# A hybrid decoder block on one core: the start re-staged with the first scale on TensorE, centring by rounded products, and another order

## The chip, the cores and the metric

The kernel runs on one core of a Trainium2 chip. The core has a matrix engine (PE, with its weight loads shown apart as PEld), a vector engine (DVE), an activation engine (ACT), a general engine (POOL) and a queue engine (SP), which here issues the loads and stores. The metric is the device time of one execution in microseconds (us); shorter is better. Three timed executions of the kernel before gave 963.92, 964.54 and 966.73 us, so its median is 964.54 us.

## The reference, cut to what matters

All arrays are fp32; there is one sequence of S = 1024 tokens and D = 1024 channels. The vector `c` conditions every stage by shifts, scales and gates.

```python
c_act = jax.nn.silu(c)
cond = c_act @ ada_w[i] + ada_b[i]
shift1, scale1, gate1, shift2, scale2, gate2 = jnp.split(cond, N_MOD, axis=-1)

h = modulate(rmsnorm(x, norm1_g[i]), shift1, scale1)      # h*(1+scale)+shift
z = h @ w_in[i] + b_in[i]                                 # 1024 -> 2048
u, v, val, gate = jnp.split(z, [D_A, 2 * D_A, 2 * D_A + D_B], axis=-1)
y_a = spatial_gating_mixer(gelu(u), gelu(v), ...)         # chunks of 128 tokens, 8 heads
y_b = conformer_conv_mixer(val, gate, ...)                # 31 taps, then a group norm, silu
y = jnp.concatenate([rmsnorm(y_a, ...), rmsnorm(y_b, ...)], axis=-1)
x = x + gate1[:, None, :] * (y @ w_out[i])

h2 = modulate(rmsnorm(x, norm2_g[i]), shift2, scale2)
g_ff, up_ff = jnp.split(h2 @ w_ffn_in[i], 2, axis=-1)     # 1024 -> 2 x 2816
x = x + gate2[:, None, :] * ((jax.nn.silu(g_ff) * up_ff) @ w_ffn_out[i])

shift_f, scale_f = jnp.split(c_act @ ada_f_w + ada_f_b, 2, axis=-1)
return modulate(rmsnorm(x, norm_f_g), shift_f, scale_f)
```

The group norm of the convolution branch subtracts, over 64 channels, the mean, and divides by the deviation. The matrix `gcen` (128x128) does the subtraction as a product: it is the identity less 1/64 within a group.

## The kernel before, in words

Channels lie on the partitions and tokens along the free axis, so `x` is eight tiles of 128 channels; the tokens are worked in two halves of 512. A product of two fp32 matrices is made of rounded parts: each operand is split into a value rounded to fp32r (`h`, `wh_...`, the "high" part) and the remainder (`wl_...`, and a second plane of `h`), and three fp32r products are added up in a bank (`mm3`, L748): high by high (L750), low weight by high (L751), high weight by low (L752). A true fp32 matrix product is used only for small things, such as sums of squares and the group norm's centring (L1090).

The stages, as the trace places them: the start (0 to 16 us: loads of `x`, the sums of squares, the first reciprocal root, the first scale and shift); phase 1 of half 0 (16 to 61 us: for k = 0 to 7 a scale, a shift, a weight tile and 24 products into eight banks `p`); the remaining input projections `u`, `vg`, `v` with the convolution of half 0, whose taps run on DVE as one multiply-add each (`cv`, L1070); the spatial gate, the branch norms and the output projection of half 0; then "ahead" products (`ah`, L1139), products of the FFN's first layer that need only half 0 and that are interleaved with the convolution and the group norms of half 1 (257 to 345 us); the output projection of half 1; a stretch in which the second half's FFN operand is prepared (385 to 446 us); the dense FFN (446 to 940 us); and the tail.

A shift or a scale column is a dot product of `c_act` with 128 rows of `ada_w`. Its usual form (`ada_cols`, L693) loads these rows as a 128x1024 tile and lets DVE multiply and sum up in one instruction (SCALAR_TENSOR_TENSOR at L703); some are done by POOL's multiply (L700) with ACT's sum (L701).

What sets the order of the work: the program is first written in plain order, and then a planner in the kernel (`fix_order`, L561) fixes the order of every engine's instructions. It holds a graph of the instructions with a duration for each, goes forward and backward through it by a list rule, and stretches every duration off PE by a margin (one factor for computing, one for DMAs). The kernel before makes twelve orders, four rounds for each of three margins, replays each four times with jittered durations, and keeps the one with the smallest sum of replayed times. Extra edges say what must come first: `in_turn` chains the first loads on SP's queue, and `issue_after` holds an instruction behind another.

The loads at the start are issued as `c_row`, four tiles of 512 KB of `x` (two channel blocks each), the first scale's rows, the first shift's rows, the first weight tile and `colt` (small columns: biases, norm gains, convolution taps). The squares of `x` are made by turns on ACT (even k) and DVE (odd k); PE sums them over the channels into `ssq_n1_0` (L890); ACT takes the root (L894), DVE the reciprocal (L895), PE spreads the row over the partitions (L897), DVE multiplies `x` by it (`t_h`, L926), and ACT applies scale and shift and rounds (`h`, L928). `keep_busy` (L873) puts idle bf16 products of 128x512 behind the sums so that PE doesn't stand still.

Around 119 us the first product of the `v` projection needs a bank that the spatial bias' sums (`rs`) still hold; the four DVE instructions at L860 read it into `bst`.

Of the kernel before, what the change touches and what calls it, by code (L numbers as in the profile page):

```python
# [13 lines left out]
P = 128  # L14
S = 1024
D = 1024
# [19 lines left out]
IDLE = (1, 1, 2, 3, 3)  # L36
# [9 lines left out]
    ("ada_b", 64), ("norm1_g", 8), ("norm2_g", 8), ("norm_f_g", 8), ("b_in", 16),  # L46
# [31 lines left out]
MARGINS = ((1.01, 1.05), (1.015, 1.075), (1.02, 1.1))  # L78
JITTER = (0.008, 0.08)
TRIALS = 4  # L80
# [421 lines left out]
def replay(g, order):  # L502

    place, done, at = dict.fromkeys(ENGINES, 0), {}, [0.0] * len(g.steps)
    need = [len(s.before) for s in g.steps]
    slots, clock, table = Slots(g), Clock(True), None
    for _ in range(len(g.steps)):
        best = None
        for e in ENGINES:
            if place[e] == len(order[e]) or need[order[e][place[e]].n]:  # L510
                continue
            s = order[e][place[e]]
            tag, t = slots.blocked_on(s)
            t = max(t, at[s.n], clock.free[e])
            if tag is None and (best is None or t < best[0]):
                best = t, s
        t, s = best
        slots.take(s)
        if s.table not in (None, table):
            table, t = s.table, t + TABLE_LOAD  # L520
        begin, end = clock.run(s, t)
        done[s.n] = end
        if slots.release(s, end + SIGNAL[s.engine]):
            slots.hand_over()
        for n in s.after:
            need[n] -= 1
            if (s.n, n) in g.turns:
                at[n] = max(at[n], t + DMA_ISSUE)
            elif g.steps[n].engine == s.engine and not s.dma:
                at[n] = max(at[n], clock.free["PE"] if s.engine == "PE" else end)  # L530
            else:
                at[n] = max(at[n], end + SIGNAL[s.engine])
        place[s.engine] += 1
    return max(done.values())


# [16 lines left out]
def jittered(g, order, seed):  # L553

    import random
    rng = random.Random(seed)
    with stretched(g, lambda s: 1 + abs(rng.gauss(0, JITTER[s.dma]))):
        return replay(g, order)


def fix_order(tc, edges, stacked, reusing, rounds=4):  # L561

    g = Graph(list(tc.nc.cur_bb.bb.instructions), edges, stacked, reusing)
    orders = []
    for margin in MARGINS:
        with stretched(g, lambda s: margin[s.dma]):
            order, done, follows = forward(g, list(range(len(g.steps))))
            for _ in range(rounds):
                tail = backward(g, [-t for t in done], follows)
                order, done, follows = forward(g, [-t for t in tail])  # L570
                orders.append(order)
    times = [sum(jittered(g, order, seed) for seed in range(TRIALS)) for order in orders]
    best = orders[times.index(min(times))]
    for steps in best.values():
# [7 lines left out]
def block_kernel(ctx: ExitStack, tc: tile.TileContext, xT, c, ada, cols, vbias, bs, wsp,  # L582
# [49 lines left out]
    c_load = nc.sync.dma_start(c_row[0:1, :], c).ins  # L632
# [19 lines left out]
    sel_tok = const.tile([P, 4], F32, name="sel_tok")  # L652
    V.memset(sel_tok, 0.0)
    for q in range(4):
        V.memset(sel_tok[32 * q:32 * q + 1, q:q + 1], 1.0)

    warm = const.tile([P, 1], F32, name="warm")
    A.activation(warm, epst, AF.Silu)
    cact = const.tile([P, D], F32, name="cact")
# [986 lines left out]
```

## Time and profile before

| what | value |
|---|---|
| timed executions | 963.92, 964.54, 966.73 us (median 964.54) |
| the profiled execution | 967.9 us, of it span 965.8 us |
| mean granted clock of PE in it | 0.995 |
| PE busy | 946.5 us, 98% of the span |
| DVE busy | 861.9 us, 89% |
| ACT busy | 482.1 us, 50% |
| POOL busy | 413.6 us, 43% |
| moved by DMA | 184.24 MB, mean 191 GB/s |

Every number of a stage comes from the profiled execution, which is 3.4 us longer than the median; the part of its time that lies outside the span is 2.1 us. A row of the timeline view gives start, duration, engine, line, operation, tiles, and in brackets how long the engine stood idle ahead of it and what released it; a row with "x3" holds three instructions one behind another. A row of the windows view gives the stretch and its length, then each engine's busy time with its instructions in it, then the clock granted to PE, the share of DMA engines busy and the GB/s. A row of the waits view gives what waited for what: total us, times, longest us.

### The profile page before, as it was taken

To read this page: it belongs to the slowest core of one execution; us is meant where nothing else is said; L and a number is where in the kernel's file an instruction comes from. 1 tells how busy PE (TensorE), PEld (TensorE's weight loads), DVE (VectorE), ACT (ScalarE), POOL (GpSimd) and SP (SyncE) were. 2 spreads that over 40 slices of the span, in tenths; PEclk is the share of its full clock that TensorE was granted. 3 is DMA by queue.
4 is the path that set the end of the run, shared out by engine and by line. 5 is a ranking of instruction groups with operands and counts; after the bars stand their busy time and mean duration, and the time that the engine had idled before them with its cause. 6 is when DMAs were issued, how large, how long until landed. Compare 5 with 4: busy or idle time off the path is not lost.

```text
span 965.8 us, 12863 instructions
## 1 busy us (share of the span) xinstructions
PE 946.5 (98%) x4461; PEld 767.1 (79%) x4461; DVE 861.9 (89%) x1226; ACT 482.1 (50%) x770; POOL 413.6 (43%) x253
## 2 busy tenths in 40 slices
PE   7999999999999999999999999999999999999996
PEld 4888777778777788887888888888888888888885
DVE  6989999999999763899999999999778989969966
ACT  6778468763474743554333333223337337227426
POOL 0069896776554403673545454554534200000132
PEclk9999999999999999999999999999999999999998
DMA  9873342443385443753677677767648848405104
GB/s 351 325 265 136 110 174 88 153 159 130 139 280 202 147 146 138 263 205 119 239 238 251 221 236 243 249 236 238 224 171 277 269 158 260 164 33 165 54 1 174
DMA packets 70498, 184.24 MB, mean 191 GB/s; under 512 B 7841, under 2 KB 8353, under 8 KB 70434
## 3 DMA queue, kind: packets, MB, share of 16 engines
q1 hardware_dynamic: 70434, 183.43, 55.0%
q8 instruction: 35, 0.57, 0.3%
q14 instruction: 29, 0.24, 0.1%
HBM read 142.24 MB, written 41.16 MB: 190 GB/s over the span
## 4 chain that ended last, share of the span: by engine, by line
PE 84%; DVE 9%; DMA 2%; ACT 2%; issue 2%; POOL 1%; SPq 0%; POOLq 0%; ACTq 0%; DVEq 0%
PE B L1139 31%; PE C L1139 18%; PE ah L1139 9%; PE A L1139 3%; PE po L752 3%; PE po L751 3%; PE po L750 3%; DVE cv L1070 2%; PE p L752 2%; PE p L750 2%; PE p L751 2%; PE v L750 2%; PE v L752 1%; DVE ada L703 1%; PE v L751 1%
## 5 line engine op out<-in xcount | busy, mean ns | idle before, releaser
L1139 PE MATMUL B<-h,w_f 128*128 128x512 f32 x816 | 189.9, 389 | 0.6 <-ACT w_f L1131 0.3
L1139 PEld LDWEIGHTS B<-h,w_f 128*128 128x128 f32 x816 | 153.1, 188 | 33.0 <-ACT w_f L1131 0.8
L1070 DVE SCALAR_TENSOR_TENSOR cv<-ypad,colt,cv 128x512 f32<-128x512 f32 x216 | 147.8, 745 | 0.3
L1139 PE MATMUL B<-fa,w_d 128*128 128x512 f32 x528 | 125.0, 389 | 0.0
L1139 PE MATMUL C<-h,w_f 128*128 128x512 f32 x528 | 123.7, 389 | 0.0
L1139 PEld LDWEIGHTS C<-h,w_f 128*128 128x128 f32 x528 | 99.1, 188 | 20.9 <-ACT w_f L1131 0.3
L1139 PEld LDWEIGHTS B<-fa,w_d 128*128 128x128 f32 x528 | 99.0, 188 | 20.9 <-DVE x L1500 0.3
L1139 PE MATMUL ah<-h,wh_a 128*128 128x512 f32 x320 | 101.3, 394 | 0.0
L1426 POOL TENSOR_TENSOR sq_nf<-sq_nf,sq_nf 128x512 f32<-128x512 f32 (+1 forms) x15 | 17.4, 1163 | 170.9 <-ACT sq_nf L1420 170.8
L1131 ACT ACTIVATE w_f<-raw_f 128x512 fp32r<-128x512 f32 x68 | 42.4, 630 | 87.8 <-PE B L1139 38.8
L734 POOL TENSOR_TENSOR wl_a<-raw_a,wh_a 128x1024 fp32r<-128x1024 f32 x20 | 49.4, 2468 | 77.0 <-ACT wh_a L733 77.0
L1131 ACT ACTIVATE w_d<-raw_d 128x512 fp32r<-128x512 f32 (+1 forms) x72 | 42.0, 593 | 80.2 <-PE B L1139 33.6
L1132 DVE TENSOR_TENSOR w_f<-raw_f,w_f 128x512 fp32r<-128x512 f32 x68 | 71.7, 1061 | 7.6 <-ACT w_f L1131 7.4
L1139 PEld LDWEIGHTS ah<-h,wh_a 128*128 128x128 f32 x320 | 59.8, 188 | 14.8 <-issue 1.7
L1383 POOL TENSOR_TENSOR x<-x,up 128x512 f32<-128x512 f32 x20 | 36.1, 1805 | 73.4 <-ACT x L1382 73.4
L1139 PE MATMUL C<-fa,w_d 128*128 128x512 f32 (+1 forms) x291 | 63.9, 370 | 0.0
L1139 PE MATMUL ah<-h,wl_a 128*128 128x512 f32 x160 | 62.3, 389 | 0.0
L1139 PEld LDWEIGHTS C<-fa,w_d 128*128 128x128 f32 x291 | 51.0, 188 | 9.2
L1132 DVE TENSOR_TENSOR fa<-a,fa 128x512 fp32r<-128x512 f32 x77 | 52.0, 712 | 1.1 <-ACT fa L1131 1.1
L1500 DVE SCALAR_TENSOR_TENSOR x<-B,cond,x 128x512 f32<-128x512 f32 x48 | 35.7, 746 | 18.0 <-PE B L1139 17.5
L1132 DVE TENSOR_TENSOR w_d<-raw_d,w_d 128x512 fp32r<-128x512 f32 (+1 forms) x72 | 50.6, 712 | 0.0
L1131 ACT ACTIVATE fa<-a 128x512 fp32r<-128x512 f32 x77 | 46.5, 626 | 7.4 <-DMA a<-acts 4.8
(271 smaller groups left out, 2106.3 us busy)
## 6 DMA issues: line engine op xcount, KB each, us to landing
acts<-x SPq DMA_DIRECT2D x77, 256.0 KB, 3.3
a<-acts SPq DMA_DIRECT2D x77, 256.0 KB, 4.0
raw_f<-wf SPq DMA_DIRECT2D x32, 512.0 KB, 4.8
ada<-ada SPq DMA_DIRECT2D x24, 512.0 KB, 3.4
x<-ada SPq DMA_DIRECT2D x24, 512.0 KB, 4.0
raw_a<-wf SPq DMA_DIRECT2D x20, 512.0 KB, 3.3
ahead<-ahead SPq DMA_DIRECT2D x40, 256.0 KB, 2.5
ypad<-ada SPq DMA_DIRECT2D x16, 512.0 KB, 6.0
```

Of the source, the lines that this page charges most:

```text
L703: V.scalar_tensor_tensor(raw, raw, 1.0, cact, op0=ALU.mult, op1=ALU.mult, accum_out=cond[:, j:j + 1])
L734: lo_eng.tensor_tensor(lo[:, cut], raw[:, cut], hi[:, cut].bitcast(F32), op=ALU.subtract)
L750: PE.matmul(acc, shi, mhi, start=start, stop=False)
L751: PE.matmul(acc, slo, mhi, start=False, stop=False)
L752: PE.matmul(acc, shi, mlo, start=False, stop=stop)
L1070: V.scalar_tensor_tensor(accs[j], src, wc, accs[j], op0=ALU.mult, op1=ALU.add)
L1131: A.activation(dst[:, 0, :], src, AF.Copy)
L1132: lo_eng.tensor_tensor(dst[:, 1, :], src, dst[:, 0, :].bitcast(F32), op=ALU.subtract)
L1139: last_mm = PE.matmul(bank[:, cols], s, m[:, cols], start=first and p == 0 and i == 0, stop=p == n - 1 and i == 2, skip_group_check=True)
L1383: G.tensor_tensor(g0, g0, up0, op=ALU.mult)
L1426: G.tensor_tensor(run, run, t, op=ALU.add)
L1500: V.scalar_tensor_tensor(x_tile(k, part), bank[:, cols], ccol(GATE2, k), x_tile(k, part), op0=ALU.mult, op1=ALU.add)
```

## The change

Six things change at once.

1. The start's loads come in another order: `x`'s first tile ahead of `c`, then a part of `colt` (now beginning with `c` as eight columns), the rest of `x` with the last tile in two halves, then the first scale's weights in a layout for PE (`ada1`), the first shift's rows, the first weight tile in two halves, and the rest of `colt`.
2. The first scale column (k = 0) is computed by PE: eight fp32 products of 32x128 with silu(c) as a column, an ACT copy of 128x128, and one product of 128x1; a DVE multiply-and-sum of 128x1024 goes.
3. Ten idle bf16 products of 128x512 stand at the front of PE; the idle products behind the sums are 26 of 32x128 where they were 10 of 128x512.
4. DVE makes the squares of k = 1, 3, 4, 5, 7 and ACT those of 0, 2, 6; the first rounded `h` is made by DVE and not by ACT; `gain` is computed early; the start's orders on DVE and ACT are fixed by edges.
5. For half 1 the group norm's centring is two fp32r products, of the rounded part `sh` (by ACT) and of the remainder `sl` (a new DVE subtraction), where it was one fp32 product of a copy made by ACT. Four tiles are concerned.
6. The planner uses one margin, 1.03 for computing and 1.1 for DMAs (before: up to 1.02 and 1.1), makes four rounds, adds a random number of spread 0.05 us from a fixed seed to the ranks of each round, and keeps the last order; the replays are gone.

```diff
-IDLE = (1, 1, 2, 3, 3)
+IDLE = (4, 6, 6, 6, 4)
+WARM_UP = 10
+BY_VECTOR = (1, 3, 4, 5, 7)
...
-MARGINS = ((1.01, 1.05), (1.015, 1.075), (1.02, 1.1))
-JITTER = (0.008, 0.08)
-TRIALS = 4
+MARGIN = (1.03, 1.1)
+ROUNDS_OF_ORDER, SPREAD, SEED = 4, 0.05, 577509
...
+    with stretched(g, lambda s: MARGIN[s.dma]):
+        order, done, follows = forward(g, list(range(len(g.steps))))
+        for _ in range(ROUNDS_OF_ORDER):
+            tail = backward(g, [-t for t in done], follows)
+            order, done, follows = forward(g, [-(t + rng.gauss(0, SPREAD)) for t in tail])
...
-    in_turn = [c_load] + [nc.sync.dma_start(xs[0][i], xT[0, i]).ins for i in range(KD // 2)]
+    early = _OFF["norm2_g"]
+    in_turn = [nc.sync.dma_start(xs[0][0], xT[0, 0]).ins, nc.sync.dma_start(c_row[0:1, :], c).ins,
+               nc.sync.dma_start(colt[:, 0:early], cols[:, 0:early]).ins]
+    in_turn += [nc.sync.dma_start(xs[0][i], xT[0, i]).ins for i in range(1, KD // 2 - 1)]
+    in_turn += [nc.sync.dma_start(xs[0][KD // 2 - 1][:, a, :], xT[0, KD // 2 - 1, :, a, :]).ins for a in range(2)]
...
-            ins = PE.matmul(first_bank(3, 0), idle[:, 0:P], idle, start=True, stop=True).ins
+            ins = PE.matmul(first_bank(3, 0)[0:32, 0:P], idle[:, 0:32], idle[:, 0:P], start=True, stop=True).ins
...
+    for _ in range(WARM_UP):
+        PE.matmul(first_bank(3, 0), idle[:, 0:P], idle, start=True, stop=True)
...
+    def first_scale():
+
+        raw = ypad[0][:, HALO:HALO + D]
+        nc.sync.dma_start(raw, ada1)
+        bank = gn_bank("scale_rows")
+        for k in range(KD):
+            q = k % 4
+            PE.matmul(bank[q * 32:(q + 1) * 32, 0:P], cact_cols[:, k:k + 1].broadcast_to([P, 32]),
+                      raw[:, k * P:(k + 1) * P], start=k < 4, stop=k >= 4)
+        rows = sb.tile([P, P], F32, tag="rt", name="scale_rows", bufs=2)
+        on["A"].append(A.activation(rows, bank[:, 0:P], AF.Copy).ins)
+        PE.matmul(bank[:, P:P + 1], rows, sel_tok[:, 4:5], start=True, stop=True)
+        return bank[:, P:P + 1]
...
-        h_hi = A.activation(h[:, 0, :], t, AF.Identity, bias=ccol(SHIFT1, k), scale=ccol(SCALE1, k)).ins
+        if k == 0:
+            h_hi = V.tensor_scalar(h[:, 0, :], t, ccol(SCALE1, k), ccol(SHIFT1, k), op0=ALU.mult, op1=ALU.add).ins
         else:
+            h_hi = A.activation(h[:, 0, :], t, AF.Identity, bias=ccol(SHIFT1, k), scale=ccol(SCALE1, k)).ins
...
         for j in js:
-            PE.matmul(bank[j], gcen, s[j], start=True, stop=True)
+            if s[j] is not None:
+                PE.matmul(bank[j], gcen, s[j], start=True, stop=True)
+                continue
+            hi, lo = (front.tile([P, H], F32R, tag="s", name=f"s{n}{half}_{j}", bufs=4) for n in "hl")
+            A.activation(hi, accs[j], AF.Copy)
+            V.tensor_tensor(lo, accs[j], hi.bitcast(F32), op=ALU.subtract)
+            PE.matmul(bank[j], gcen_r, hi, start=True, stop=False)
+            PE.matmul(bank[j], gcen_r, lo, start=False, stop=True)
```

DVE at the start, before: from the last square to the first remainder of `h`. `ypad` are the tiles in which the first scales' and shifts' rows land, `rt_n` the roots, `x_0` the first tile of `x`.

```order
L886 TENSOR_TENSOR sq_n_0_7_171<-x_3_78 128x512
L703 SCALAR_TENSOR_TENSOR ypad_108,cond<-ypad_108,cact 128x1024
L895 RECIPROCAL rt_n_0_180<-rt_n_0_180 128x128
L703 SCALAR_TENSOR_TENSOR ypad_109,cond<-ypad_109,cact 128x1024
L926 TENSOR_TENSOR t_h_0_0_208<-x_0_75,ssq_n_0_123 128x512
L919 SCALAR_TENSOR_TENSOR gain<-colt 128x8
L734 TENSOR_TENSOR wl_k_199<-raw_k_196,wh_k_198 128x512 x2
L703 SCALAR_TENSOR_TENSOR ypad_110,cond<-ypad_110,cact 128x1024
L933 TENSOR_TENSOR h_0_0_210<-t_h_0_0_208,h_0_0_210 128x512
```

The same place now:

```order
L852 TENSOR_TENSOR sq_n_0_7_201<-x_3_77 128x512
L863 RECIPROCAL rt_n_0_213<-rt_n_0_213 128x128
L665 SCALAR_TENSOR_TENSOR ypad_116,cond<-ypad_116,cact 128x1024
L909 TENSOR_TENSOR t_h_0_0_242<-x_0_74,ssq_n_0_142 128x512
L922 TENSOR_SCALAR h_0_0_256<-t_h_0_0_242,cond 128x512
L698 TENSOR_TENSOR wl_k_248<-raw_k_244,wh_k_247 128x512 x2
L933 TENSOR_TENSOR h_0_0_256<-t_h_0_0_242,h_0_0_256 128x512
L665 SCALAR_TENSOR_TENSOR ypad_117,cond<-ypad_117,cact 128x1024
```

The scale's multiply-and-sum no longer stands between the last square and the reciprocal, the first `h` is made on DVE, and its remainder comes ahead of the next scale.

DVE at the spatial bias, before. `cv` are the taps' sums of the convolution of half 0, two tiles at a time; `s` holds the six taps of each tile that ACT multiplies and POOL adds up.

```order
L1070 SCALAR_TENSOR_TENSOR cv_0_1214<-ypad_108,colt,cv_0_1214 128x512
L1070 SCALAR_TENSOR_TENSOR cv_1_1215<-ypad_109,colt,cv_1_1215 128x512
L1070 SCALAR_TENSOR_TENSOR cv_0_1214<-ypad_108,colt,cv_0_1214 128x512
L1070 SCALAR_TENSOR_TENSOR cv_1_1215<-ypad_109,colt,cv_1_1215 128x512
L1079 TENSOR_TENSOR s_0_1210<-s_0_1210,cv_0_1214 128x512
L1079 TENSOR_TENSOR s_1_1211<-s_1_1211,cv_1_1215 128x512
L1073 TENSOR_SCALAR cv_2_1530<-ypad_110,colt 128x512
L1073 TENSOR_SCALAR cv_3_1531<-ypad_111,colt 128x512
L860 SCALAR_TENSOR_TENSOR bst<-rs,colt,bst 128x128 x4
```

The same place now:

```order
L826 SCALAR_TENSOR_TENSOR bst<-rs,colt,bst 128x128 x4
L1071 SCALAR_TENSOR_TENSOR cv_0_1261<-ypad_115,colt,cv_0_1261 128x512
L1071 SCALAR_TENSOR_TENSOR cv_1_1262<-ypad_116,colt,cv_1_1262 128x512
L1071 SCALAR_TENSOR_TENSOR cv_0_1261<-ypad_115,colt,cv_0_1261 128x512
L1071 SCALAR_TENSOR_TENSOR cv_1_1262<-ypad_116,colt,cv_1_1262 128x512
L1080 TENSOR_TENSOR s_0_1257<-s_0_1257,cv_0_1261 128x512
L1080 TENSOR_TENSOR s_1_1258<-s_1_1258,cv_1_1262 128x512
L1074 TENSOR_SCALAR cv_2_1577<-ypad_117,colt 128x512
L1074 TENSOR_SCALAR cv_3_1578<-ypad_118,colt 128x512
```

The four instructions at the spatial bias now stand ahead of the last four taps, the two additions and the two first taps of the next pair: eight instructions earlier.

PE at the group norm of half 1 (first pair), before, among the ahead products:

```order
L1090 MATMUL gn_0_2935<-s_0_2865,cstt 128x512
L1139 MATMUL ah_0_2372<-h_0_2_2259,wh_a_2368 128x512
L1139 MATMUL ah_0_2372<-h_0_3_2266,wh_a_2368 128x512
L1139 MATMUL ah_0_2372<-h_0_3_2266,wl_a_2369 128x512
L1139 MATMUL ah_0_2372<-h_0_3_2266,wh_a_2368 128x512
L1090 MATMUL gn_1_2936<-s_1_2866,cstt 128x512
```

The same place now:

```order
L1147 MATMUL ah_0_2419<-h_0_3_2313,wh_a_2415 128x512
L1095 MATMUL gn_0_2976<-sh_0_2978,gcen_r 128x512
L1096 MATMUL gn_0_2976<-sl_0_2979,gcen_r 128x512
L1095 MATMUL gn_1_2977<-sh_1_2984,gcen_r 128x512
L1096 MATMUL gn_1_2977<-sl_1_2985,gcen_r 128x512
L1147 MATMUL ah_0_2434<-h_0_4_2320,wh_a_2415 128x512
```

Two fp32 products with ahead products between them have become four fp32r products in a row.

More of the change, by code (lines that the diff above doesn't have):

```diff
@@ L499, in backward @@
     return tail
[L502 to L534, printed above, removed]
 @contextmanager
@@ L550, in stretched, with fix_order @@
             s.bytes = size
-def jittered(g, order, seed):
+def fix_order(tc, edges, stacked, reusing):
     import random
[L556 to L561, printed above, removed]
+    rng = random.Random(SEED)
     g = Graph(list(tc.nc.cur_bb.bb.instructions), edges, stacked, reusing)
[L564 to L574, printed above, removed]
+    with stretched(g, lambda s: MARGIN[s.dma]):
[3 more added lines that the diff above has]
+            order, done, follows = forward(g, [-(t + rng.gauss(0, SPREAD)) for t in tail])
+    for steps in order.values():
         for earlier, later in zip(steps, steps[1:]):
@@ L893, in first_rstd @@
         rt = sb.tile([P, P], F32, tag="rt", name="rt_n1_0", bufs=2)
-        A.activation(rt, bank[:, 0:P], AF.Sqrt, bias=epst, scale=1.0 / D)
+        on["A"].append(A.activation(rt, bank[:, 0:P], AF.Sqrt, bias=epst, scale=1.0 / D).ins)
         last["rstd"] = V.reciprocal(rt, rt).ins
+        on["V"].append(last["rstd"])
         for q in range(4):
@@ new lines, in block_kernel @@
+        if k == 0:
+            on["V"].append(h_hi)
+            kinds = [[i for i in nc.cur_bb.bb.instructions[behind:] if i.engine == e and type(i).__name__ != "InstDMACopy"]
+                     for e in (nc.vector.engine, nc.scalar.engine)]
+            on["V"] += [i for i in kinds[0] if i not in on["V"]]
+            rounded = [i for i in kinds[1] if i not in (scaled, shifted)]
+            on["A"] += [scaled, *rounded[:1], shifted, *rounded[1:], A.activation(r1a, r1a_bank, AF.Copy).ins]
```

79 lines of the change are left out of this document (48 added, 31 removed).

## The prediction

> **What bounds the kernel now.** First the page's head, for the share of each engine.
>
> ```profile
> span 965.8 us, 12863 instructions
> PE 946.5 (98%) x4461; PEld 767.1 (79%) x4461; DVE 861.9 (89%) x1226; ACT 482.1 (50%) x770; POOL 413.6 (43%) x253
> ```
>
> PE is busy for 98%, so a gain must either take work off PE or close one of its few gaps. To see where these lie I cut the span into stages (windows view: stretch, length, busy time of PE, PEld, DVE, ACT, POOL with their counts, granted clock, DMA share, GB/s).
>
> ```profile
> 0.00:16.27 16.27, 11.30 (x86) 5.23 (x86) 8.79 (x22) 9.30 (x18) 0.49 (x8) 1.00 0.87 339
> 58.00:119.00 61.00, 61.00 (x299) 49.20 (x299) 59.81 (x78) 42.55 (x64) 53.51 (x32) 1.00 0.44 155
> 119.00:127.00 8.00, 5.88 (x19) 4.40 (x18) 8.00 (x16) 4.78 (x7) 8.00 (x5) 0.79 0.58 200
> 257.00:345.00 88.00, 87.77 (x412) 68.31 (x411) 77.81 (x120) 57.01 (x86) 38.36 (x21) 1.00 0.56 198
> 385.00:446.00 61.00, 60.42 (x282) 48.35 (x271) 55.32 (x64) 33.92 (x57) 39.02 (x20) 1.00 0.58 201
> 446.00:940.00 494.00, 494.00 (x2180) 408.77 (x2179) 449.82 (x623) 192.28 (x326) 159.87 (x101) 1.00 0.58 196
> 940.00:966.00 26.00, 16.69 (x118) 15.15 (x116) 16.81 (x36) 17.36 (x37) 8.10 (x8) 0.86 0.44 162
> ```
>
> The FFN (446 to 940 us) has no gap: 494.00 of 494.00. A product there costs 494/2180 = 0.227 us. What can be won lies at the start, around 119 us, and in small waits. The waits view names them (us in total, times, longest).
>
> ```profile
> PE v L750 <- DVE bst L860: 2.1, 1, 2.1
> PE p L750 <- ACT h L928: 1.7, 1, 1.7
> PE p L752 <- DVE h L933: 1.0, 1, 1.0
> PE pm L1013 <- DVE ya L1019: 0.8, 1, 0.8
> PE ssq_b L805 <- DVE rt_b L799: 0.6, 1, 0.6
> ```
>
> **The start.** The timeline from the last square of x to the first rounded product:
>
> ```profile
> 9.38 0.69 DVE L886 TENSOR_TENSOR sq_n<-x 128x512 f32<-128x512 f32 x1 [0.56 <-DMA x<-xT]
> 10.65 1.23 DVE L703 SCALAR_TENSOR_TENSOR ypad<-ypad,cact 128x1024 f32<-128x1024 f32 x1 [0.58 <-DMA ypad<-ada]
> 11.04 0.37 ACT L894 ACTIVATE rt_n<-ssq_n,epst 128x128 f32<-128x128 f32 x1 [1.04 <-PE ssq_n L890]
> 11.80 0.95 DVE L895 RECIPROCAL rt_n<-rt_n 128x128 f32<-128x128 f32 x1
> 12.81 1.16 PE L897 MATMUL ssq_n<-rt_n,sel_tok 128*128 128x128 f32 x8 [0.86 <-DVE rt_n L895]
> 14.00 0.69 DVE L926 TENSOR_TENSOR t_h<-x,ssq_n 128x512 f32<-128x512 f32 x1 [0.17 <-PE ssq_n L897]
> 15.41 0.81 ACT L928 ACTIVATE h<-t_h,cond 128x512 fp32r<-128x512 f32 x1
> 16.27 0.50 PE L750 MATMUL p<-h,wh_k 128*128 128x512 f32 x1 [1.66 <-ACT h L928]
> 18.86 1.89 DVE L926 TENSOR_TENSOR t_h<-x,r_n 128x512 f32<-128x512 f32 x3
> 20.67 1.22 DVE L734 TENSOR_TENSOR wl_k<-raw_k,wh_k 128x1024 fp32r<-128x1024 f32 x1
> 22.95 0.68 DVE L933 TENSOR_TENSOR h<-t_h,h 128x512 fp32r<-128x512 f32 x1
> 23.68 0.50 PE L752 MATMUL p<-h,wh_k 128*128 128x512 f32 x1 [1.01 <-DVE h L933]
> ```
>
> The reciprocal (11.80) stood behind the scale's multiply-and-sum (10.65 to 11.88), although its root was there at 11.41; and ACT's scale, shift and rounding took from 14.69 to 16.22. The change removes both. With the same bytes ahead of the last tile of x, the last square again ends near 10.07. The tile's first half now lands earlier, so only the last four sums are left: root at 10.6 to 11.0, reciprocal to 11.95 (0.95), spreading to 13.2 (1.16 and the hand-over), `t_h` to 13.9 (0.69), and `h` on DVE to about 14.4 (no row of this kind; between 0.35, half of a 0.69 pass, and 0.81, ACT's; I take 0.5). The new products for the scale need ada1, which lands where the first scale's rows did (10.65); eight small products, a copy and a column product, at most the 1.16 of the spreading and two ACT passes of 0.37, end by 12.6, ahead of `t_h`. The load order's cost is none as long as x's last tile isn't later: the shift's multiply (1.23, now behind the reciprocal) ends by 13.2. So the first product comes at 14.4, 1.9 earlier.
>
> PE cannot keep all of that. From `t_h` at 13.2, DVE's order runs 0.69 + 0.5 + weight remainder 1.22 (two halves) + remainder of `h` 0.68 + scale 1.23 + `t_h` 0.69 + shift 1.23 + three `t_h` 1.89 + weight remainder 1.22 + scale 1.2 + remainder 0.68, which ends at 24.4 where it ended at 23.63. But by PE's order the remainder of `h` for k = 1 is now wanted after 36 products and not after 26 as before (its reader at 23.68, with the wait of 1.0), so PE has 10 x 0.227 = 2.3 done more and starts 0.8 later: a gain of **1.5** (ends 2.5 and 0). The extra idle products lie in this stage's gaps (16.27 less 11.30); without that cover they would cost 26 times a quarter of 0.227, 1.5.
>
> **The stall at 119 us.** The timeline there, DVE and POOL, then PE:
>
> ```profile
> 106.15 6.59 DVE L703 SCALAR_TENSOR_TENSOR ada<-ada,cact 128x1024 f32<-128x1024 f32 x1
> 112.67 5.36 DVE L1070 SCALAR_TENSOR_TENSOR cv<-ypad,colt,cv 128x512 f32<-128x512 f32 x8
> 117.94 1.27 DVE L1079 TENSOR_TENSOR s<-s,cv 128x512 f32<-128x512 f32 x2
> 119.13 1.39 DVE L1073 TENSOR_SCALAR cv<-ypad,colt 128x512 f32<-128x512 f32 x2
> 120.44 1.11 DVE L860 SCALAR_TENSOR_TENSOR bst<-rs,colt,bst 128x128 f32<-128x128 f32 x4
> 105.65 1.31 POOL L1065 TENSOR_TENSOR s<-s,cp 128x512 f32<-128x512 f32 x1
> 106.90 4.76 POOL L734 TENSOR_TENSOR wl_v<-raw_v,wh_v 128x1024 fp32r<-128x1024 f32 x2
> ```
>
> The multiply-and-sum took 6.59 us where the same form took 1.23 at the start, and it ended with POOL's three back-to-back instructions (105.65 to 111.66) and its own 1.2 behind them. All behind it came 5.4 late, `bst` too, for which PE's `v` product waits. The stretch 119 to 127 held 19 products, worth 19 x 0.227 = 4.3 us of its 8.00: a loss of **3.7**, of it 2.1 the wait and the rest products at a granted clock of 0.79. In the new order `bst` stands ahead of eight instructions, four taps (half of 5.36), 1.27 and 1.39, together 5.3 us. It ends near 116 even if the starving stays, ahead of the time at which PE asks (119.4). I take the whole 3.7; ends 4 and -1 (the waiting moves on).
>
> [...]
>
> **Two small waits.** `pm` on `ya` (0.8) and `ssq_b` on `rt_b` (0.6): the order has three to four taps fewer (0.67 each by the 5.36 row) ahead of both on DVE. Gain **1.4**; ends 1.4 and -1.
>
> **The centring.** The chain has a row for one fp32 product of this kind and one for the products beside it; the tile view gives a DVE instruction of the new one's form.
>
> ```profile
> 268.50 0.86 PE gn L1090 x2
> 271.15 19.33 PE ah L1139 x84
> L1115 DVE TENSOR_TENSOR s<-s,gn x8: 675/680/689, 161.0 to 337.0; 128x512 f32<-128x512 f32 x8
> ```
>
> Two fp32r products take 2 x 19.33/84 = 0.46, so four tiles save 4 x (0.86 - 0.46) = **1.6** on PE, which is the bound there. The price is four subtractions of 0.68 = 2.7 us on DVE. ACT's rounding replaces its copy. In the stage (257 to 345) DVE has 88.00 - 77.81 = 10 us free, so they fit; but the second pair's stand between the last tap and the norm that PE's output projection waits for at the end of the stage, and PE's ahead products cover only part of them. I take **+0.5** (ends -0.5 and 3, the whole 2.7).
>
> **What the new order brings late.** In the FFN the reading of the order shows one place with less lead: three instructions more (2.0 us) come ahead of an `fa` remainder.
>
> ```profile
> 743.26 5.29 DVE L1132 TENSOR_TENSOR fa<-a,fa 128x512 fp32r<-128x512 f32 x5
> 747.66 2.43 PE L1139 MATMUL A<-fa,w_d 128*128 128x512 f32 x10
> ```
>
> PE reads there (747.66) while that DVE row still runs (to 748.55); taken one by one, the smallest lead of a remainder over its reader is 0.55, so up to 2.0 - 0.55 = 1.4 can be lost: **+0.6** (ends 0 and 1.4). At 443 us the loss of 385 to 446 is only 61.00 - 60.42 = 0.6, and one DVE multiply moves out ahead: 0 (ends -0.6 and 3). In the tail, where PE is busy for 16.69 of 26, the order is nearly the same: **+0.3** (ends -0.5 and 1).
>
> **The sum:** -1.5 - 3.7 - 1.4 - 1.6 + 0.5 + 0.6 + 0.3 = -6.8. Against the profiled execution, 967.9 (span 965.8 and 2.1 around it), that is 961.1; it stands 3.4 above the median of 964.54, against which the sum gives 957.7. The 119 stall hangs on a chance meeting of DVE and POOL, so the quicker executions may not have had all of it. I take between the two, **959.0**.
>
> **Rivals.**
> A. The stall stays: the multiply-and-sum, only one pair of taps earlier on DVE, meets the same three POOL instructions, and POOL's later weight remainder, which now comes behind one more multiply of its own, is late for PE. 959 + 3.7 = 962.7. For it: POOL is busy for 53.51 of the 61 us before. Against: `bst` has 5.3 us more room. Chance 0.17.
> B. The start does not do what it says: the smaller idle products leave PE at a low clock for the first products. After 119 us the records stood 0.43 apart for a stretch; eight such products cost 8 x 0.2 = 1.6, the whole gain: 960.5. Against: the granted clock was 1.00 in the first stage with PE busy for 11.30. Chance 0.1.
>
> ```profile
> 122.76 0.63 PE L751 MATMUL v<-wh_v,h 128*128 128x512 f32 x1
> 123.19 0.63 PE L752 MATMUL v<-wl_v,h 128*128 128x512 f32 x1
> ```
>
> [...]
>
> C. Slower: the preparation of the second half (385 to 446) lengthens. DVE is busy for 55.32 and POOL for 39.02 of 61 there, so one more meeting as at 106 us costs 5.4 on DVE, and only 5.7 is free. From two meetings on PE waits for them: 959 + 2 x 5.4 = 969.8. Against: the order takes a multiply out of this stretch. Chance 0.17.
> The forecast itself has 0.56.
>
> **The numbers.** 0.3% of the median, 2.9 us, is about what a measurement of this kernel can tell from no change: faster is below 961.6, slower above 967.4. The forecast's own range is 954 (every term at its good end: 2.5 + 4 + 1.4 + 1.6 + 1.1 off the median) to 962; with A and B the range 954 to 966 holds 0.83. Faster: 0.56 + 0.1, and 0.01 of A = 0.67. Same: 0.16. Slower: C, 0.17.
>
> **What would show it.** Right: the first rounded product near 14.4 us and its `h` made by DVE; no wait on the spatial bias' instruction near 117 us and a clock of 1.00 there; eight short products where four fp32 ones were; PE busy falling by some 2 us. Wrong: PE's waits listing `sl` or the deviation near 325 us, a DVE multiply-and-sum of several us ahead of a wait in 385 to 446, or new waits in the FFN, where now there are none.

## The result, and the profile after

The changed kernel takes 961.45 us (median of nine executions, 961.05 to 964.27); the kernel before, timed beside it, 966.73 us (nine executions, 963.92 to 968.75). The ratio is 0.9953, with a 95% interval of 0.994 to 0.9967: faster by about 0.5%. The forecast was 959.0 in a range of 954 to 966. The three executions of before that the prediction had in hand lay low: in the 64 later ones that stand beside the experiments the medians are 966.1 to 967.2, so the profiled execution of 967.9 lies nearer to the usual one than the median of those three does. One of the 64 took 1360.5 us at a granted clock of 0.655 and the ratios leave it out.

The head of the profile page after (span 962.3 us, this execution took 964.27):

```profile
span 962.3 us, 12994 instructions
PE 947.2 (98%) x4505; PEld 769.7 (80%) x4505; DVE 859.0 (89%) x1234; ACT 478.8 (50%) x771; POOL 411.0 (43%) x253
```

PE's busy time rose by 0.7 in this execution, with the new idle products in it. That is its late start (see below): in a second profiled execution of the same kernel (961.46 us, span 959.5) PE is busy for 944.4, which is 2.1 less than before and what the prediction named. There PE stands idle for 15.1 us where it was 19.3 before, so the larger part of the gain is in the gaps. The windows view of the first execution, for the stretches shown of before:

```profile
0.00:16.27 16.27, 14.26 (x117) 7.51 (x118) 5.55 (x20) 6.68 (x12) 0.49 (x8) 1.00 0.86 320
58.00:119.00 61.00, 59.66 (x291) 47.54 (x290) 54.10 (x81) 41.02 (x61) 54.91 (x32) 1.00 0.48 170
119.00:127.00 8.00, 8.00 (x37) 6.63 (x36) 8.00 (x13) 4.63 (x7) 7.57 (x4) 1.00 0.41 135
257.00:345.00 88.00, 87.01 (x416) 69.02 (x415) 83.26 (x128) 55.35 (x84) 36.66 (x20) 1.00 0.57 196
385.00:446.00 61.00, 61.00 (x273) 49.31 (x272) 58.31 (x64) 35.93 (x59) 35.52 (x21) 1.00 0.60 200
446.00:940.00 494.00, 494.00 (x2185) 409.16 (x2184) 448.32 (x624) 189.53 (x324) 159.54 (x102) 1.00 0.57 195
```

The stretch from 119 to 127 us is full now (37 products where there were 19, clock 1.00), and the gap of 385 to 446 is gone. Two stretches got worse: 58 to 119 us, which had no gap, lost 1.3, and 257 to 345 us has a gap of 1.0 where it had 0.2. The waits view after names what PE waits for:

```profile
PE pu L715 <- POOL wl_u L698: 1.3, 1, 1.3
PE p L714 <- DVE h L922: 1.1, 1, 1.1
PE ssq_nf L1420 <- POOL sq_nf L1434: 1.0, 1, 1.0
PE ssq_nf L1452 <- DVE rt_nf L1450: 1.0, 1, 1.0
PE gn L1122 <- DVE late L649: 0.5, 1, 0.5
PE ah L1147 <- ACT h L731: 0.5, 1, 0.5
```

The waits on `bst` (2.1), `ya` (0.8) and `rt_b` (0.6) are gone; one on a weight remainder of the u projection (1.3), one on POOL's squares in the tail (1.0), and a small one on ACT's `h`, are new, and the one on `late` has grown (before 0.2). In the tail the wait on `rt_nf` has shrunk (before 1.9).

To place all this in time, the same product was looked up in two profiled executions, and its start in the one taken from its start in the other. The table gives the median of these differences over a stretch of before's time. A row is one execution, a minus is earlier than in before's profile, and a step between two columns is what the stretch between them won or lost. `after_again` is a second profiled execution of the changed kernel (961.46 us); the other rows are the experiments.

```
us of before       24-40   90-105  127-140  225-257  300-315  360-385  500-700  956-966
after               +2.4     +4.3     +0.3     -1.6     -1.9     -2.3     -3.2     -3.4
after_again         -0.4     +1.5     -2.5     -4.4     -4.7     -5.1     -6.0     -6.2
no_warm_up          -0.1     +1.8     -2.2     -4.0     -4.4     -4.7     -5.6     -5.8
no_idle             -0.3     +1.0     -3.0     -4.8     -5.1     -5.5     -6.4     -6.6
c_first             -0.8     +1.1     -2.9     -4.7     -5.1     -5.4     -6.4     -6.6
fp32_centring       -0.3     +1.6     -2.4     -4.3     -4.6     -4.9     -5.9     -6.1
old_planner         +1.8     +3.1     +0.0     +0.1     -0.2     -0.5     -1.4     -1.8
new_planner         -0.3     +1.0     -3.0     -4.2     -4.5     -3.5     -4.3     -4.4
bst_early           +0.1     +0.1     -2.3     -1.6     -1.5     -1.5     -1.6     -1.6
pool_swap           +2.3     +8.8     +4.8     +3.0     +2.6     +2.2     +1.3     +1.1
pool_one            -0.2     +1.1     -2.9     -4.7     -5.1     -5.4     -6.3     -6.5
seed_1              +0.0     +0.6     -3.4     -4.6     -5.0     -5.3     -6.3     -5.5
no_spread           +2.4     +4.3     +0.3     +2.1     +1.9     +2.4     +1.5     +1.3
```

By the row of `after_again` the start won 0.4, the u projection lost 1.9, the stretch around 119 us won 4.0, that around 200 us 1.9, the centring's stretch 0.3, 315 to 385 us 0.4, 385 to 500 us 0.9, and the tail 0.2. Rows are to be compared with rows of a like start: `after`, `old_planner`, `pool_swap` and `no_spread` show executions with a late start (first column +1.8 to +2.4).

### The profile page after: what moved, and what is told of

Read it like the earlier page. It is cut to its first block, busy times and chain, and to the rows that moved or that the text cites. A ratio compares the mean times of both kernels' runs of the same rounds, so it can differ in the third digit from the quotient of the medians.

```text
span 962.3 us, 12994 instructions
## 1 busy us (share of the span) xinstructions
PE 947.2 (98%) x4505; PEld 769.7 (80%) x4505; DVE 859.0 (89%) x1234; ACT 478.8 (50%) x771; POOL 411.0 (43%) x253
## 4 chain that ended last, share of the span: by engine, by line
PE 89%; DVE 5%; issue 2%; POOL 2%; ACT 1%; ACTq 0%; POOLq 0%; DVEq 0%
PE B L1147 32%; PE C L1147 18%; PE ah L1147 11%; PE A L1147 4%; PE po L714 3%; PE po L715 3%; PE po L716 3%; PE v L714 2%; PE v L715 2%; PE v L716 2%; PE p L714 1%; PE p L715 1%; PE pu L715 1%; PE p L716 1%; PE pu L716 1%
## 5 line engine op out<-in xcount | busy, mean ns | idle before, releaser
L1140 DVE TENSOR_TENSOR w_f<-raw_f,w_f 128x512 fp32r<-128x512 f32 x68 | 68.3, 1018 | 1.8 <-ACT w_f L1139 1.8
L1394 POOL TENSOR_TENSOR x<-x,u 128x512 f32<-128x512 f32 x22 | 39.4, 1791 | 46.8 <-DVE u L1393 46.8
L1391 POOL TENSOR_TENSOR x<-x,up 128x512 f32<-128x512 f32 x20 | 30.9, 1544 | 42.3 <-ACT x L1390 42.2
L1140 DVE TENSOR_TENSOR w_d<-raw_d,w_d 128x512 fp32r<-128x512 f32 (+1 forms) x72 | 48.5, 685 | 0.1
```

The costliest lines, as they stand in the source:

```text
L1140: lo_eng.tensor_tensor(dst[:, 1, :], src, dst[:, 0, :].bitcast(F32), op=ALU.subtract)
L1391: G.tensor_tensor(g0, g0, up0, op=ALU.mult)
L1394: G.tensor_tensor(g1, g1, u2, op=ALU.mult)
```

## The experiments

Twelve kernels ran. In those that keep the changed kernel's order (or before's), the order is written into the kernel as a list, so that one thing alone moves; where the planner runs anew, every engine's order may change, and this is said.

### The start: a control, no idle products ahead, none at all

The changed kernel again, and two kernels with its order:

```diff
-WARM_UP = 10
+WARM_UP = 0
```

and, for the third, `-IDLE = (4, 6, 6, 6, 4)` `+IDLE = (0, 0, 0, 0, 0)` as well.

> The changed kernel itself, as a control beside the next three: a time near its median of 961.45 us (961 to 964.3), and the first rounded product near 18.9 us as in its first profile. Its start is 2.6 us later than before's (18.89 against 16.27 us), where the prediction said 1.9 earlier; the three theories of that are tested by the next two runs.

> The changed kernel without its ten idle products at the front of PE; every other instruction stands in the same order. Theory 1 (the ten idle products, 1.29 to 5.3 us on PE, hold up c's two products, and with them silu, ACT's change to the root's table and all behind): c's products at 2.5 to 4.2 us, the first rounded product 2 to 2.8 us earlier (16.1 to 16.9), the time 2 to 2.8 us shorter. Theory 2 (PE is filled by the 26 idle products between the sums): at most 0.5 us shorter. Theory 3 (the loads' new order: x's second tile is squared at 7.33 us, where it was at 5.80): no change.

> As the run without the ten idle products, and also without the 26 small ones behind the sums; every other instruction stands in the same order. Theory 2 (the small ones take PE's time between the sums): 1 to 2 us shorter than without the ten alone. Theory 1: within 0.5 us of it. If the clock needs the idle products: a granted clock under 1.00 in the first microseconds of rounded products, their starts 0.43 us apart and not 0.23, and 1.5 to 3 us longer.

Measured: 961.78 us for the control (961.34 to 962.2), 962.28 without the ten (961.77 to 963.29), 962.09 without any idle product (960.92 to 963.26). None differs from the others by more than its own spread. Theories 1 and 2, which expected 1 to 2.8 us, fail; theory 3 expected no change here and is tried in the next experiment.

What happened at the start is seen by setting the changed kernel's two profiles beside each other. First profile (964.27 us), timeline:

```profile
1.29 4.02 PE L872 MATMUL p<-idle 128*128 128x512 bf16 x9 [1.29 <-DVE sel_tok L611]
5.24 3.78 PE L624 MATMUL c<-c_row,ones 1*128 1x512 f32 x4
9.05 0.60 ACT L625 ACTIVATE cact<-c 128x512 f32<-128x512 f32 x1 [1.11 <-PE c L624]
14.67 0.37 ACT L862 ACTIVATE rt_n<-ssq_n,epst 128x128 f32<-128x128 f32 x1 [2.46 <-PE ssq_n L858]
18.89 0.97 PE L714 MATMUL p<-h,wh_k 128*128 128x512 f32 x3 [1.11 <-DVE h L922]
```

Control (961.46 us), the same rows:

```profile
1.29 3.64 PE L872 MATMUL p<-idle 128*128 128x512 bf16 x9 [1.29 <-DVE sel_tok L611]
4.85 1.98 PE L624 MATMUL c<-c_row,ones 1*128 1x512 f32 x4
6.87 0.60 ACT L625 ACTIVATE cact<-c 128x512 f32<-128x512 f32 x1 [0.26 <-PE c L624]
8.56 2.11 DVE L852 TENSOR_TENSOR sq_n<-x 128x512 f32<-128x512 f32 x3 [0.59 <-DMA x<-xT]
11.82 0.37 ACT L862 ACTIVATE rt_n<-ssq_n,epst 128x128 f32<-128x128 f32 x1 [1.80 <-PE ssq_n L858]
16.05 0.96 PE L714 MATMUL p<-h,wh_k 128*128 128x512 f32 x3 [1.11 <-DVE h L922]
```

The instructions and their order are the same; c's four passes took 3.78 us in one and 1.98 in the other, and everything behind them is 2.8 us apart. Without the ten idle products ahead they took 3.75 (in before, `no_warm_up`, `no_idle` and `c_first` alike), so behind the ten they ran at about twice that pace in the one execution and not in the other; what decides between the two is not shown. Of the changed kernel's 15 executions only the two of 963.8 us and more lie that far off, so most seem to have the quick start. That the loss of 2.4 in the first profile (row `after`, first column) is a matter of the executions and not of the change is seen from the second. The control's granted clock doesn't stay up either: it reads 1.00 up to 7.0 us, 0.62 under the sums (from 7.0 to 10.5 us in the windows view), 0.90 from 10.5 to 14.0 us, and 1.00 from there to 21.0 us.

```profile
7.00:10.50 3.50, 3.50 (x64) 2.56 (x60) 2.51 (x4) 2.99 (x5) 0.00 (x0) 0.62 1.04 399
```

Without any idle product:

```profile
4.22 3.75 PE L777 MATMUL c<-c_row,ones 1*128 1x512 f32 x4 [4.22 <-DMA c_row<-c]
16.18 0.97 PE L867 MATMUL p<-h,wh_k 128*128 128x512 f32 x3 [1.43 <-DVE h L1075]
16.98 0.62 PE L868 MATMUL p<-h,wl_k 128*128 128x512 f32 x2
```

c's passes run slowly here (3.75), but they begin as soon as c lands (4.22), and nothing else is in PE's way; the first product comes at 16.18. The rounded products are not slowed as the `v` products of before were after the wait at 119 us (0.43 apart): the first three start 0.27 apart (0.80 us up to the next at 16.98), the next two 0.23 (to 17.44). So the idle products gain about what they cost: c's passes are quicker by 1.8 but begin 0.6 later, and the 26 small ones stand between the sums (without the ten alone the first rounded product comes at 16.38, without all at 16.18). Rival B (a slow clock at the first rounded products) did not come true, even without any idle product.

### The loads' order

The kernel without idle products, with c's load first again and the small columns behind x's second tile (order of SP only):

```diff
-x0, c_row, colt[:, :80], x1, x2, x3 in halves
+c_row, x0, x1, colt[:, :80], x2, x3 in halves
```

> The run without any idle product, and with c's load ahead of x's first tile and the first columns of colt behind x's second tile; all else in the same order. Theory 3 (the loads' new order delays the start: c lands at 4.2 us where it landed at 2.4, x's second tile is squared at 7.2 where it was at 5.8): c's products at 2.5, the first rounded product 0.8 to 1.6 us earlier than without idle products (16.18), so 14.6 to 15.4, and 960.5 to 961.3 us for 962.09. If the start is bound elsewhere (ACT's change of tables, PE's sums): within 0.3 us of it.

Measured: 962.41 us (961.1 to 964.86).

```profile
2.43 3.75 PE L777 MATMUL c<-c_row,ones 1*128 1x512 f32 x4 [2.43 <-DMA c_row<-c]
10.02 0.69 DVE L1005 TENSOR_TENSOR sq_n<-x 128x512 f32<-128x512 f32 x1 [0.30 <-DMA x<-xT]
15.72 0.96 PE L867 MATMUL p<-h,wh_k 128*128 128x512 f32 x3 [1.44 <-DVE h L1075]
```

c's products begin at 2.43 and the first rounded product at 15.72, 0.5 earlier than without this (16.18); theory 3 expected 0.8 at least. And the 0.5 is not there at the end: in the table both rows arrive at the same -6.6, since 0.6 of it (from -0.8 to +1.1, where `no_idle` goes from -0.3 to +1.0) is lost again at 77 us, where the wait on POOL's weight remainder is 1.3 us again. PE only comes earlier to the same wait; why POOL's remainder does not come earlier by as much was not followed up. The last square (10.02 to 10.71) is still 0.6 later than before's (9.38 to 10.07): the new load order, with the first columns of `colt` ahead of x's last tile and that tile in halves, brings it later and not earlier; which of the two does it was not tried.

### The centring by one fp32 product

```diff
-            A.activation(hi, accs[j], AF.Copy)
-            V.tensor_tensor(lo, accs[j], hi.bitcast(F32), op=ALU.subtract)
-            PE.matmul(bank[j], gcen_r, hi, start=True, stop=False)
-            PE.matmul(bank[j], gcen_r, lo, start=False, stop=True)
+            A.activation(hi, accs[j], AF.Copy)
+            PE.matmul(bank[j], gcen, hi, start=True, stop=True)
```

(with `hi` in fp32), all else in the changed kernel's order.

> The changed kernel with half 1's centring by one fp32 product per tile again (without the four subtractions on DVE and one of the two products), all else in the same order. If the centring is worth what the prediction says: PE's time in 257 to 345 us 1.6 us longer (4 x 0.4), and 1 to 1.6 us in the whole. If the four subtractions cost as much as the products save: no change or shorter.

Measured: 961.59 us (961.43 to 963.74), no different from 961.78. The windows view of the stretch, first with one fp32 product per tile, then the control:

```profile
257.00:345.00 88.00, 88.00 (x414) 68.93 (x413) 81.08 (x124) 56.63 (x86) 36.68 (x20) 1.00 0.55 192
```

```profile
257.00:345.00 88.00, 87.01 (x415) 68.78 (x414) 83.19 (x126) 56.84 (x86) 36.67 (x20) 1.00 0.56 192
```

The rounded products do take work off PE, but its busy time falls only into idleness: 88.00 becomes 87.01. Where one piece of it goes is seen at the first pair. One fp32 product per tile:

```profile
264.99 1.88 PE L1247 MATMUL gn<-sh,cstt 128*128 128x512 f32 x4
266.50 0.60 PE L1298 MATMUL ah<-h,wh_a 128*128 128x512 f32 x1
```

Two rounded products per tile:

```profile
264.88 0.39 PE L1095 MATMUL gn<-sh,gcen_r 128*128 128x512 f32 x1
265.57 0.39 PE L1096 MATMUL gn<-sl,gcen_r 128*128 128x512 f32 x1
266.40 0.50 PE L1147 MATMUL ah<-h,wh_a 128*128 128x512 f32 x1 [0.45 <-ACT h L731]
```

The four rounded products start 0.23 apart and the next could start near 265.8; but it needs an `h` that ACT has at 266.4, and starts there, 0.1 ahead of the kernel with the slow products. Of the second pair's saving most goes into the wait on `late` (0.5). What is left of 1.6 is 0.1 to 0.2 by the traces, and nothing by the times.

### The planner

The changed kernel with before's planner, and the kernel before with the new planner (everything planned anew in both):

```diff
-MARGIN = (1.03, 1.1)
-ROUNDS_OF_ORDER, SPREAD, SEED = 4, 0.05, 577509
+MARGINS = ((1.01, 1.05), (1.015, 1.075), (1.02, 1.1))
+JITTER = (0.008, 0.08)
+TRIALS = 4
```

> The changed kernel's instructions, put in order by the planner of before (three margins, four rounds each, the best of twelve in replays). If the gain comes from the new order: 964 to 967 us, as before, and a wait of PE on DVE or POOL between 60 and 260 us of 3 us or more in all. If it comes from the instructions themselves (start, centring): 960 to 962.5 us.

> The kernel before, put in order by the new planner (one margin 1.03 and 1.1, ranks with a random part, the last order kept). If the gain comes from the new settings as such: 961 to 963 us. If the gain hangs on the one order that this seed gives with the changed instructions: anywhere from 962 to 970, since the same random numbers fall on other instructions.

Measured: 963.46 us (962.61 to 966.23), ratio to before 0.9971 (0.9956 to 0.9986); and 963.74 us (962.72 to 964.73), ratio 0.9966 (0.9954 to 0.9978). The first lies between its two expected ranges. Each gives about 0.3%, and both together 0.5%. Before's instructions in the new planner's order already win the 4.0 us around 119 (row `new_planner`, +1.0 to -3.0) and lose 1.0 at 345 to 360 us. The changed instructions under the old planner win 3.1 around 119 as well, without the new margins: a new order is also made by new instructions.

Two more kernels ask whether the margins or the draw make it:

```diff
-ROUNDS_OF_ORDER, SPREAD, SEED = 4, 0.05, 577509
+ROUNDS_OF_ORDER, SPREAD, SEED = 4, 0.05, 1
```

and the same with spread 0.0 and the seed as it was.

> The changed kernel, its planner with another seed for the random part of the ranks. If the margins make the order good: 961 to 963 us. If the order of this one seed was a lucky draw: 963 to 970 us, with waits of PE at other places than in the changed kernel.

> The changed kernel, its planner without the random part (spread 0), the margins as changed. If the margins alone make the gain: 961 to 963 us. If the random part with this seed makes it: 963 to 970 us.

Measured: 962.81 us (961.88 to 964.54), ratio 0.997 (0.9957 to 0.9984), with the other seed; 966.21 us (964.11 to 969.19), ratio 0.9996 (0.9984 to 1.0009), without the random part: no gain at all, with the same instructions and the same margins. Its waits view names what its order makes late:

```profile
PE gn L1122 <- DVE gd L649: 1.6, 1, 1.6
PE po L714 <- ACT y_b L1029: 1.6, 1, 1.6
PE pu L715 <- POOL wl_u L698: 1.3, 1, 1.3
```

So the margins alone are not the cause, and the instructions alone aren't either. The gain is in the particular order; two draws of two gave one, which says that they are not rare, and not how often they come. The table shows where the orders differ. All five newly planned ones win the stretch around 119 us (3.1 us in `old_planner`, 4.0 in the others), `no_spread` too: its row is that of `after` up to 140 us. Behind that, up to 257 us, `after` wins 1.9 and `no_spread` loses 1.8.

### The stall at 119 us: one part of the move alone

The kernel before, in its own order, with only the four instructions of the spatial bias moved ahead of the eight that the new order puts behind them:

```diff
-cv0 cv1 cv0 cv1 s0 s1 cv2 cv3 bst bst bst bst
+bst bst bst bst cv0 cv1 cv0 cv1 s0 s1 cv2 cv3
```

> The kernel before in its own order, but for the four DVE instructions of the spatial bias, which stand eight instructions earlier (where the changed kernel has them). If the wait at 119 us is the largest single part of the gain: no wait of PE on them, a granted clock of 1.00 in 119 to 127 us, and 3.5 to 4 us shorter than before; so about half to all of what the whole change gives. If the wait only moves to the next one (the v products' weights on POOL, or the convolution): under 1.5 us.

Measured: 966.52 us (964.14 to 969.65), ratio 1.0003 (0.9988 to 1.0018). The wait on `bst` is gone and the clock stays up, and yet nothing is gained:

```profile
119.00:127.00 8.00, 6.68 (x29) 5.20 (x29) 8.00 (x14) 4.96 (x7) 8.00 (x5) 1.00 0.57 191
```

```profile
PE v L901 <- POOL wl_v L883: 1.3, 1, 1.3
PE v L899 <- ACT vn L1124: 0.5, 1, 0.5
```

```profile
106.24 6.61 DVE L852 SCALAR_TENSOR_TENSOR ada<-ada,cact 128x1024 f32<-128x1024 f32 x1
115.41 1.11 DVE L1009 SCALAR_TENSOR_TENSOR bst<-rs,colt,bst 128x128 f32<-128x128 f32 x4
116.28 2.41 POOL L849 TENSOR_TENSOR ada<-ada,cact 128x1024 f32<-128x1024 f32 x1 [4.52 <-DVE cv L1219]
118.64 2.43 POOL L883 TENSOR_TENSOR wl_v<-raw_v,wh_v 128x1024 fp32r<-128x1024 f32 x1
```

PE now waits 1.3 us for the third weight remainder of v. POOL makes it at 118.64, behind a multiply before which POOL stood idle for 4.52 us. The idle time ends with one of DVE's taps, which stand behind the multiply-and-sum, long as in before (6.61 us, where the form took 1.23 at the start of before; this is the starving of the prediction): it holds up DVE, DVE holds up POOL's multiply, and the remainder stands behind that. In the changed kernel the multiply-and-sum itself is short:

```profile
104.58 2.56 DVE L665 SCALAR_TENSOR_TENSOR ada<-ada,cact 128x1024 f32<-128x1024 f32 x1
113.00 1.12 DVE L826 SCALAR_TENSOR_TENSOR bst<-rs,colt,bst 128x128 f32<-128x128 f32 x4
106.00 3.42 POOL L698 TENSOR_TENSOR wl_v<-raw_v,wh_v 128x1024 fp32r<-128x1024 f32 x1
112.98 2.41 POOL L662 TENSOR_TENSOR ada<-ada,cact 128x1024 f32<-128x1024 f32 x1
```

It takes 2.56 us and POOL's multiply begins at 112.98 and not at 116.28. Here it was POOL's next remainder that took longer: 3.42 us, where the one at 118.64 above took 2.43. So the stall had two arms, DVE's and POOL's. That it goes with their common cause is argued, since no run takes away the starving alone; `old_planner` bears it out. There the multiply-and-sum isn't starved, `bst` stands behind taps and additions again, and the stretch still wins 3.1 us:

```profile
111.23 1.22 DVE L712 SCALAR_TENSOR_TENSOR ada<-ada,cact 128x1024 f32<-128x1024 f32 x1
118.83 1.12 DVE L873 SCALAR_TENSOR_TENSOR bst<-rs,colt,bst 128x128 f32<-128x128 f32 x4
```

By its profile this kernel is 1.6 us earlier at the end than before's profile, while the medians are equal; before's executions differ by up to 5 us among themselves, and its one profile (967.9) is 1.2 above their median. How large the stall is in a typical execution of before was not seen. The mean granted clocks give a hint: 0.996 to 0.997 in before's executions of 966.5 to 967.1 us, 0.993 to 0.995 in those above 967.8, to which the profiled one belongs. A clock of 0.79 over 8 us is worth 1.7 us (8 x 0.21), or 0.002 of the mean, so the middle executions may have had the wait without the lowered clock.

### The new wait at 77 us

In the changed kernel two additions on POOL stand between and ahead of the weight remainders of u. Both were moved behind the third remainder, then only the second of them; all else in the same order.

```diff
 wl_u_1
-s0_0<-cp0_0_1
 sq_n1_1_6
-s0_1<-cp0_1_1
 wl_u_2
+s0_0<-cp0_0_1
+s0_1<-cp0_1_1
 wl_u_3
```

> The changed kernel with two additions on POOL (first convolution products of tiles 0 and 1) put behind the third weight remainder of the u projection, all else in the same order. In the changed kernel PE waits 1.3 us for that remainder near 77 us, a wait that before has not. If the two additions are its cause: the wait gone and 1 to 1.3 us shorter, 960.3 to 960.7. If it moves (the fourth remainder, or the convolution, late instead): no shorter.

> The changed kernel with only one of the two additions on POOL (tile 1's) put behind the third weight remainder of u. With both, ACT's next product for the convolution waited 4.7 us for a buffer that an addition frees, and the fourth rounding of u stood behind it on ACT. With one, ACT's next product has its buffer. If that explains the loss: PE's wait near 77 us gone and 0.5 to 1.3 us shorter than the changed kernel, 960.3 to 961. If any shift there costs: 963 or more.

Measured: 966.58 us (965.47 to 968.8) for both, ratio to before 0.9995 (0.9981 to 1.0009), where the changed kernel's control had 0.9952: the whole gain lost; and 961.07 us (960.58 to 963.21) for the one, ratio 0.9954 (0.994 to 0.9968). With both:

```profile
77.62 0.72 ACT L1218 ACTIVATE cp<-ypad,colt 128x512 f32<-128x512 f32 x1 [4.70 <-POOL s L1219]
78.95 1.04 ACT L850 ACTIVATE wh_u<-raw_u 128x1024 fp32r<-128x1024 f32 x1
```

```profile
PE pu L867 <- ACT wh_u L850: 3.4, 1, 3.4
```

ACT makes the products that POOL adds, into two buffers. With both additions late, both buffers stay full, ACT waits 4.70 us, and the rounding of u's fourth weight, which PE needs next, is queued behind that wait on ACT. The wait of 3.4 isn't the whole loss: the granted clock falls with it, to 0.53 in 79 to 86 us, where 15 products start in 7 us:

```profile
79.00:86.00 7.00, 5.95 (x15) 4.71 (x16) 4.29 (x6) 6.54 (x9) 5.93 (x5) 0.53 0.41 142
```

With one addition late a buffer is free, and the wait on the third remainder goes; part of it comes back as another wait, 0.8 (in the table 1.3 is still lost up to 90 us, where the control loses 1.9):

```profile
PE pu L869 <- POOL h L885: 0.8, 1, 0.8
```

That version has the lowest median of all that ran, 0.4 us under the changed kernel, but by the ratio it is no different from it.

## Why the prediction was right, and which of its steps were not

The forecast (faster by 5.5 us off the median then known) and its range held: the measured ratio is worth 4.5 us. The sum, -6.8 against before's profile, stands beside -6.2 in `after_again`. That is partly luck: the start and the centring gave 2.5 us less than forecast and 1.9 were lost where nothing was expected, while three forecast costs of 1.4 in all did not come and 0.9 was won at 443 us.

- **The start, -1.5: mis-sized.** Measured -0.4 in the control, and +2.4 in the first profile, where c's passes took 3.78 us. The removed steps are gone: the reciprocal follows its root directly, and `h` takes 0.55 on DVE (I took 0.5). But the root comes at 11.82 and not at 10.6. Two steps failed. The last square was to end at 10.07 as before, with "the same bytes ahead" of it, but the first columns of `colt` now load ahead of that tile too, and it ends at 10.67. And the halved tile was to bring the root 0.5 behind the last square; it comes 1.15 behind it, where before it was 0.97. Another 0.4 is lost behind the root (4.23 us to the first product, forecast 3.8). That the idle products cost nothing was right on balance: without any of them the root comes at 11.96. But they don't lie in gaps, as the prediction had it; they stand among the sums and make up for that with c's quicker passes (1.98 us against 3.75).
- **The stall at 119, -3.7: right in place and size, wrong in cause.** -4.0 in `after_again`. The step that failed is that moving `bst` alone removes it, even if the starving stays: that was tried, and by the times it gained nothing (by the one profile 1.6). The new order shortens the starved instruction to 2.56 us and brings POOL's chain forward too. Rival A, that the starving stays, did not come true; its second half, a late remainder on POOL, is what the move alone runs into.
- **The two small waits, -1.4: right.** -1.9 between 140 and 257 us, and both are gone from the waits. That fewer taps ahead are the reason was not tried alone.
- **The centring, -1.6: failed.** 0.1 to 0.2. The products' costs were read well (the rounded ones start 0.23 apart), but "PE is the bound there" was not true at the place: 0.6 us behind the first pair PE needs an operand of ACT.
- **330 to 350 us, +0.5, 747 us, +0.6, 443 us, 0:** the first two costs did not come (-0.4 between 315 and 385; no wait in the FFN), and the third was a gain of 0.9. The tail gave 0.2.
- **Not foreseen: +1.9 at the u projection.** The order of POOL was compared around 119 us only. The third remainder of u now stands behind an addition, and PE waits 1.3 for it; where the other 0.6 goes was not followed up.

Rival C (a longer preparation of the second half) did not happen: that stretch has no gap at all.

## What to carry to other kernels

When engines have fixed orders, the cost of a move is set by what is queued behind each instruction on every engine, including buffers that a late instruction keeps full: here moving two additions by a few places cost the whole gain (966.58 us), moving one cost nothing (961.07). Work taken off the busiest engine can fall into idleness, as the centring's did here (PE's busy time in its stretch went from 88.00 to 87.01 us, the time from 961.59 to 961.78), if the next operand isn't there yet; look for the next wait behind the place before counting it. Of an order that a planner draws, measure several, since the same instructions ran between 961 and 967 us here.

## What the runs showed of the hardware that was not expected

- The granted clock in the profile reads 1.00 in the first microseconds also where products run at half pace: c's passes took 3.78 us in one execution of the changed kernel and 1.98 in another, with the same instructions, and the column shows 1.00 from 0 to 7 us for both.
- A DVE multiply-and-sum that ran beside POOL's tensor-tensor instructions took 6.59 and 6.61 us in the two kernels with before's order, where the same form took 1.23 at the start of before; it ended after several of them. In the two profiles of the changed kernel it took 2.66 and 2.56 us, and the POOL remainder that began during it took 3.40 and 3.42 where others there take 2.4. In `old_planner` it took 1.22. What decides this is not shown.
- Two waits of PE went with a lowered clock, and more was lost than their length. With the wait of 2.1 us the granted clock was 0.79 over 119 to 127 us (before; without that wait the changed kernel's control won 4.0 us there). With the wait of 3.4 us it was 0.53 over 79 to 86 us (`pool_swap`, which lost 6.5 us between the first two columns of the table, where `after` lost 1.9). With the waits of 1.3 us it read 1.00 over the same stretches (119 to 127 in `bst_early`, 79 to 86 in the first profile of the changed kernel).
